# Input projection in seven block products per pair of feature tiles, five down-projection blocks and four input buffers in the mixer, in a one-core encoder layer

## The chip, the cores and the metric

One core of a Trainium2 chip runs the whole layer in one launch. The metric is the device time of an execution in microseconds; the comparison goes by the median of several runs. All arithmetic is in fp32; a matmul in full precision is made from three matmuls in fp32r (a rounded form), each operand being split into a rounded part `hi` and a rest `lo` (hi·hi + hi·lo + lo·hi).

## The reference

2176 frames (2048 of a prompt, and 8 sequences of 16 sample frames) of 1024 features go through one layer:

```python
h = rms_norm(x, g_mix_pre)
qa, ka, va, qb, kb, vb, ga, gb = split(h @ w_in)          # 1024 -> 4352 columns
qa, ka = rope(qa), rope(ka)
oa = attention A (8 query heads, 2 key heads, window of 2 chunks back, sinks)
ob = attention B (8 heads, 8 chunks back, relative-position bias)
mixed = sigmoid(ga) * (oa @ w_oa) + sigmoid(gb) * (ob @ w_ob)
x = x + rms_norm(mixed @ w_out, g_mix_post)
h = rms_norm(x, g_ffn_pre)
u, val = split(h @ w_up)                                  # 1024 -> 2 * 2816
ff = (gelu(causal_conv3(u)) * val) @ w_down               # 2816 -> 1024
x = x + rms_norm(ff, g_ffn_post)
```

The outputs are the frames, and new keys, values and convolution rows.

## The kernel before, in words

Features lie on partitions, frames on the free axis. A matmul multiplies a weight tile of 128x128 with up to 512 frames and adds into a PSUM bank; `mm3` (L127 to L131) issues the three fp32r matmuls of one 128-deep step. `split` (L133) makes `hi` on ScalarE (ACT, L134) and `lo` on VectorE (DVE, L135). All loads and nearly all stores are issued on SyncE's (SP's) one queue.

The stages, in order:

1. **Input projection** (L180 to L373). The 4352 output columns are 34 tiles of 128 (`u`): 0 to 4 values, 5 and 6 to 9 the keys and queries of mixer A (with `rope`), 10 to 13 keys and 14 to 17 queries of mixer B, 18 to 33 the gates. The frames stand in five groups of 512, 512, 512, 384 and 256 (`GROUPS`). The raw frames are split; the weights are scaled by `g_mix_pre` while they are split (`unit` with `g`, L154, L155); the reciprocal norm `rs` multiplies the result when it leaves PSUM (`project`, L196). Each `u` and group takes 8 steps of 128, which are 24 matmuls. The gates of the last two groups (`LATE`, 640 frames) are left for the attention. An evacuated tile of keys or queries is rotated (L324 to L327), scaled (L345), split into `hi` and `lo` (one buffer each) and stored with four DMAs (L304, L312).
2. **Attention** (L378 to L778). Its matmuls are interleaved with those of the late gates as filler (`late_gates`), 256 steps of three matmuls: `F0` of them at the start, `FD` at each of 32 places of the sample part, `F1` after it, the rest by a share, `FE` of which are kept for the end.
3. **Mixer and output projection** (L783 to L960): per frame group, eight tiles `od` are loaded and split (`ot`, two buffers, L816), and eight weight units of `wo` follow; then `w2`.
4. **Up projection** (L963 to L1077). Pairs of feature tiles (gate and value) and two halves of a frame block form a 2x2 block product, made with **seven** block products: `stationary` makes sums of weight tiles on GpSimd (POOL, L982 to L985), `moving` makes sums of frames, `seven` runs 7 products of 12 matmuls over 364 frames in the order `ORDER` into three PSUM banks, and combinations on ACT and DVE give the four results.
5. **Down projection** (L1081 to L1155): six half blocks of 364 or 360 frames (`halves`); per block 22 tiles `gx` are loaded and split into `ghl` (33 buffers), and for each of 8 output tiles 22 steps run; the weights are loaded and split anew for each block. `finish_half` normalises and stores.

The order in which instructions stand on each engine is chosen by a scheduler when the program is built. It keeps each engine's queue in one order; an engine waits at the instruction that stands next.

```python
GROUPS = [(0, 512), (512, 512), (1024, 512), (1536, 384), (1920, 256)]
...
for u in range(3, 34):
    w = wp.unit(i["w1"][u], g=gv[:, 0])
    for g in range(5):
        if u < 18 or g not in LATE:
            evac(u, g, project(w, g, psm, ev))
```

## Time and profile before

| | before |
|---|---|
| median of 3 runs | 3182.87 us (3181.53 to 3184.79) |
| profiled execution | 3180.94 us, span 3178.9 us |
| busy: PE / DVE / ACT / POOL | 3067.4 / 2013.1 / 1391.3 / 517.8 us |
| PE busy, share of the span | 96% |
| mean granted TensorE clock | 0.988 |
| bytes moved | 463.39 MB, mean 146 GB/s |

PE is TensorE's matmul, PEld its weight load. The PE duration of a matmul includes its way through the array, so that neighbours overlap; what a matmul costs is the distance from its start to the next one's. A granted clock of 1.00 is TensorE's upper level of 2.4 GHz, 0.50 the lower of 1.2 GHz. A time behind `<-` is idle time of an engine and what ended it.

### The profile page before, as it was taken

The page shows a single profiled execution, that of the slowest core. Times are in us where ns is not written, and L with a number is a line of the kernel's source. Part 1 is how long each engine was busy: PE and PEld are TensorE (multiplying, and loading weights), DVE is VectorE, ACT ScalarE, POOL GpSimd, SP SyncE. Part 2 cuts the span into 40 slices and gives each one's busy share as a digit, 9 for nine tenths or more (in the row PEclk, how much of TensorE's full clock was granted, in tenths as well). Part 3 has the DMA queues.
Part 4 walks back from the last instruction along what each step waited for, and adds up shares of the span by engine and source line. Part 5 has one row for each costly group of instructions (what it writes and reads, how often), then busy time and mean ns, then how long its engine had stood idle before and what let it go on. Part 6 is the DMA issues. An engine that isn't in the chain of part 4 may idle for free.

```text
span 3178.9 us, 49235 instructions
## 1 busy us (share of the span) xinstructions
PE 3067.4 (96%) x18387; PEld 2810.9 (88%) x18387; DVE 2013.1 (63%) x3769; ACT 1391.3 (44%) x2724; POOL 517.8 (16%) x442
## 2 busy tenths in 40 slices
PE   7999999999999999999979998999989999999997
PEld 6888888888787776899969998999989999999997
DVE  7365442224587665556888878887887775555554
ACT  6264222223587663134444444444444434444432
POOL 0000000001121100000024344434544430000000
PEclk9999999999999999999999999999999999999998
DMA  6366642227766636654533222322222236666764
GB/s 182 93 173 176 142 117 83 82 81 249 236 182 175 169 101 195 217 167 130 155 119 114 105 96 89 126 106 97 86 93 105 103 114 213 217 209 203 213 183 134
DMA packets 253943, 463.39 MB, mean 146 GB/s; under 512 B 29824, under 2 KB 130056, under 8 KB 253704
## 3 DMA queue, kind: packets, MB, share of 16 engines
q1 hardware_dynamic: 249352, 446.62, 45.8%
q0 software_dynamic: 4352, 13.64, 1.2%
q8 instruction: 144, 2.36, 0.3%
q14 instruction: 95, 0.78, 0.1%
HBM read 344.98 MB, written 115.15 MB: 145 GB/s over the span
## 4 chain that ended last, share of the span: by engine, by line
PE 74%; DVE 10%; POOL 5%; ACT 4%; issue 3%; DMA 3%; SPq 0%; POOLq 0%; ACTq 0%; DVEq 0%
PE psm L129 20%; PE psm L131 20%; PE psm L130 19%; PE pso L698 4%; PE pst L715 3%; PE pss L653 2%; POOL ws L983 2%; DMA x<-in_xT 1%; DVE wlo L135 1%; DVE cv L1044 1%; POOL ws L985 1%; POOL ws L982 1%; POOL ws L984 1%; ACT sw L324 1%; PE psf L129 1%
## 5 line engine op out<-in xcount | busy, mean ns | idle before, releaser
L135 DVE TENSOR_TENSOR wlo<-wraw,whi 128x1024 fp32r<-128x1024 f32 (+1 forms) x226 | 300.8, 1332 | 329.6 <-ACT whi L134 328.7
L134 ACT CAST whi<-wraw 128x1024 fp32r<-128x1024 f32 (+1 forms) x226 | 226.9, 1005 | 449.8 <-PE psm L130 325.4
L129 PE MATMUL psm<-hh,whi 128*128 128x512 f32 (+2 forms) x1104 | 408.6, 370 | 12.1 <-ACT hh L134 10.8
L130 PE MATMUL psm<-hl,whi 128*128 128x512 f32 (+2 forms) x1104 | 408.9, 370 | 1.6 <-DVE hl L135 1.6
L131 PE MATMUL psm<-hh,wlo 128*128 128x512 f32 (+2 forms) x1104 | 408.4, 370 | 0.0
L129 PE MATMUL psm<-ghl,whi 128*128 128x364 f32 (+1 forms) x1056 | 349.2, 331 | 2.6 <-ACT ghl L134 2.6
L130 PE MATMUL psm<-ghl,whi 128*128 128x364 f32 (+1 forms) x1056 | 346.5, 328 | 2.1 <-DVE ghl L135 2.1
L131 PE MATMUL psm<-ghl,wlo 128*128 128x364 f32 (+1 forms) x1056 | 347.1, 329 | 0.4 <-DVE wlo L135 0.4
L129 PEld LDWEIGHTS psm<-hh,whi 128*128 128x128 f32 x1104 | 208.6, 189 | 44.4 <-ACT hh L134 10.8
L196 DVE TENSOR_TENSOR f<-psm,rs 128x512 f32<-128x512 f32 (+2 forms) x138 | 87.6, 637 | 245.4 <-PE psm L131 242.5
L130 PEld LDWEIGHTS psm<-hl,whi 128*128 128x128 f32 x1104 | 208.4, 189 | 34.1 <-DVE hl L135 2.1
L131 PEld LDWEIGHTS psm<-hh,wlo 128*128 128x128 f32 x1104 | 208.5, 189 | 32.3 <-issue 0.5
L129 PEld LDWEIGHTS psm<-ghl,whi 128*128 128x128 f32 x1056 | 199.3, 189 | 4.4 <-ACT ghl L134 3.5
L130 PEld LDWEIGHTS psm<-ghl,whi 128*128 128x128 f32 x1056 | 199.1, 189 | 3.3 <-DVE ghl L135 2.7
L131 PEld LDWEIGHTS psm<-ghl,wlo 128*128 128x128 f32 x1056 | 199.4, 189 | 0.7 <-DVE wlo L135 0.7
L982 POOL TENSOR_TENSOR ws<-wraw 128x512 f32<-128x512 f32 x66 | 93.6, 1419 | 564.4 <-DVE wlo L135 438.8
L154 ACT ACTIVATE whi<-wraw,gv 128x128 fp32r<-128x128 f32 x400 | 126.7, 390 | 96.4 <-PE psm L130 75.6
L129 PE MATMUL psm<-mhi,whi 128*128 128x272 f32 x512 | 150.7, 294 | 0.0
L131 PE MATMUL psm<-mhi,wlo 128*128 128x272 f32 x512 | 148.1, 289 | 0.0
L130 PE MATMUL psm<-mlo,whi 128*128 128x272 f32 x512 | 147.6, 288 | 0.0
L1044 DVE SCALAR_TENSOR_TENSOR cv<-ue,cw,cv 128x728 f32<-128x728 f32 (+1 forms) x132 | 130.9, 991 | 2.4 <-ACT cv L1041 1.1
L655 DVE CUSTOM_DVE_ANT_0 pB<-pss,bt 128x640 f32<-128x640 f32 (+4 forms) x128 | 93.8, 737 | 54.9 <-PE pss L653 36.8
(268 smaller groups left out, 8042.8 us busy)
## 6 DMA issues: line engine op xcount, KB each, us to landing
wraw<-in_wu SPq DMA_DIRECT2D x132, 512.0 KB, 3.9
wraw<-in_wd SPq DMA_DIRECT2D x96, 512.0 KB, 3.8
wraw<-in_w SPq DMA_DIRECT2D x58, 512.0 KB, 3.9
keys<-kd SPq DMA_DIRECT2D x80, 256.0 KB, 4.4
wraw<-in_wd SPq DMA_DIRECT2D x48, 384.0 KB, 3.3
q<-qd SPq DMA_DIRECT2D x64, 256.0 KB, 3.8
gd<-cv SPq DMA_DIRECT2D x44, 364.0 KB, 2.3
gx<-gd SPq DMA_DIRECT2D x88, 182.0 KB, 4.1
```

The source lines that it names most:

```text
L129: TE.matmul(ps, lhsT=hi, rhs=xhi, start=first, stop=False, skip_group_check=more)
L130: TE.matmul(ps, lhsT=hi, rhs=xlo, start=False, stop=False, skip_group_check=more)
L131: TE.matmul(ps, lhsT=lo, rhs=xhi, start=False, stop=last, skip_group_check=more)
L134: S.copy(out=hi, in_=src)
L135: E.tensor_sub(out=lo, in0=src, in1=hi.bitcast(F32))
L154: S.activation(out=hi[:, k], in_=r[:, k], func=AF.Copy, scale=g[:, k:k + 1])
L196: V.tensor_mul(out=f, in0=ps, in1=rs[:, t0:t0 + n])
L655: V.tensor_tensor_reduce(out=pj[:, a:], in0=ps[:, off + a:off + 640], in1=bt_[p, hf][:, a:], op0=ALU.add, op1=ALU.min, scale=1.0, scalar=3 ...
L698: TE.matmul(ps_o[hf * HD:(hf + 1) * HD, q0 * P:(q0 + nq) * P], lhsT=v[:, hf * HD:(hf + 1) * HD], rhs=tsb[hf][:, col:col + nq * P], start=( ...
L715: TE.transpose(out=tp[:, col:col + P], in_=u["P"][hf][j][:, bl * P:(bl + 1) * P], identity=ident)
L982: G.tensor_add(out=s1, in0=r1[:, 0:4], in1=r1[:, 4:8])
L1044: V.scalar_tensor_tensor(out=cv[:, :npr], in0=ue[:, s_:s_ + npr], scalar=cw[:, f, s_:s_ + 1], in1=cv[:, :npr], op0=ALU.mult, op1=ALU.add)
```

## The change

1. The input projection is made of the same seven block products as the up projection. Two feature tiles (`u`, `u + 1`) and two halves of a frame block form a pair. The blocks are 2 x 384, 2 x 384 and 2 x 320 frames (`IBLOCKS`). The four value tiles 0 to 3 of the first block are made directly, as before (`DIRECT`), while the block's frames are prepared. Pairs of blocks 0 and 1 cover all 34 tiles, those of block 2 tiles 0 to 17; its gates stay late, over two halves of 320 frames (`LATES`).
2. The frames are scaled by `g_mix_pre` and the reciprocal norm in the staging (`squares`, `norm`, `scale`), so weights are split without a scale and results leave PSUM without one. `moving1` makes the seven sums of frames.
3. Stores are cut at multiples of 512 frames (`segments`), since the scratch tensors are still in chunks of 512. `hi`, `lo`, `cs`, `sn`, `sw` have one buffer each, `f` has five.
4. The down projection has five blocks, four of 464 and one of 320 frames (`DBLOCKS`), 27 buffers `ghl`, six `xh`; `gd` is one tensor per feature tile.
5. The mixer's `ot` has four buffers. The filler is spread by `F0, FD, F1, FE = 64, 3, 4, 56` (72, 3, 8, 40 before).

`stationary` and `seven` move to the front of the program; `seven` gets its PSUM pool and order as arguments. The core of the diff:

```diff
-F0, FD, F1, FE = 72, 3, 8, 40
+F0, FD, F1, FE = 64, 3, 4, 56
+DBLOCKS = [(0, 464), (464, 464), (928, 464), (1392, 464), (1856, 320)]
+DW = 464
-GBUFS = 33
+GBUFS = 27
 ORDER = ((1, 0), (6, 1), (5, 2), (7, 1), (2, 0), (4, 1), (3, 2))
+IBLOCKS = [(0, 384), (768, 384), (1536, 320)]
+IORDER = ((1, 0), (5, 2), (6, 1), (7, 1), (2, 0), (4, 1), (3, 2))
+DIRECT = 4
+LATES = ((1536, 320), (1856, 320))
...
+        def store_q(h0, h1, t0, n, hi, lo):
+            for t, m, c in segments(t0, n):
+                if t >= SEQ:
+                    continue
+                for hf, h in ((0, h0), (1, h1)):
+                    for z, x in ((0, hi), (1, lo)):
+                        dma(out=qd[h][t // 512][z * HD:(z + 1) * HD, t % 512:t % 512 + m],
+                            in_=x[hf * HD:(hf + 1) * HD, c:c + m].bitcast(F32))
...
+        def stage(bi):
+            b0, n = IBLOCKS[bi]
+            hs, ss, r = tiles_of(bi)
+            for c0 in range(0, 2 * n, P):
+                piece(hs, b0, c0)
+            yield hs
+            for c0 in range(0, 2 * n, P):
+                squares(hs, c0, ss)
+                yield hs
+            for z in range(2):
+                norm(ss, z * n, n, r)
+            yield hs
+            for k in range(0, KD, 2):
+                scale(hs, 0, 2 * n, r, (k, k + 1))
+                yield hs
...
+        def moving1(hs, n, pool_of, extra):
...
+            put(1, b11)
+            V.tensor_sub(out=b11, in0=b12, in1=b11)
+            put(5, b11)
+            yield x
+            V.tensor_sub(out=b11, in0=b22, in1=b11)
+            put(6, b11)
+            if extra:
+                put(0, b12)
+            G.tensor_sub(out=b12, in0=b22, in1=b12)
+            put(7, b12)
+            put(2, b21)
+            G.tensor_sub(out=b11, in0=b21, in1=b11)
+            put(4, b11)
+            put(3, b22)
+            yield x
...
+            def ready(z, ps):
+                if z == 0:
+                    S.copy(out=s1, in_=ps[0])
+                elif z == 2:
+                    V.tensor_add(out=q, in0=ps[1], in1=s1)
+                elif z == 3:
+                    V.tensor_add(out=t, in0=ps[1], in1=s1)
+                    f = tile_f()
+                    V.tensor_add(out=f, in0=ps[2], in1=t)
+                    evac(u + 1, tb, n, f)
+                elif z == 4:
+                    f = tile_f()
+                    S.copy(out=f, in_=ps[0])
+                    evac(u, ta, n, f)
+                elif z == 5:
+                    f = tile_f()
+                    V.tensor_add(out=f, in0=ps[1], in1=s1)
+                    evac(u + 1, ta, n, f)
+                elif z == 6:
+                    f = tile_f()
+                    V.tensor_add(out=f, in0=ps[2], in1=q)
+                    evac(u, tb, n, f)
+            seven(w, x, n, ready, psm, IORDER)
...
-            nxt = wp.unit(i["w1"][18], g=gv[:, 0])
+            nxt = wp.unit(i["w1"][18])
...
-        op = ph.enter_context(tc.tile_pool(name="p3i", bufs=2, reuse_waits="tile"))
+        op = ph.enter_context(tc.tile_pool(name="p3i", bufs=4, reuse_waits="tile"))
...
-        for z, (bi, hf) in enumerate(halves):
+        for z, (t0, n) in enumerate(DBLOCKS):
```

The scheduler lays the instructions out anew. Three places follow; a tile's name stands ahead of the arrow, what it is made from behind it.

SP's queue, in the tiles of mixer A's queries (`cs` and `sn` are the rotation's factors, `qd` the stored queries, `wraw` a weight tile that comes in). Before:

```order
L319 DMA cs<-in_cos 128x512
L320 DMA sn<-in_sin 128x512
L304 DMA qd_1_61<-hi 64x512
L304 DMA qd_1_61<-lo 64x512
L304 DMA qd_1_77<-hi 64x512
L304 DMA qd_1_77<-lo 64x512
L319 DMA cs<-in_cos 128x384
L320 DMA sn<-in_sin 128x384
```

In the changed kernel, two results of a pair of the first block:

```order
L299 DMA cs<-in_cos 128x384
L300 DMA sn<-in_sin 128x384
L189 DMA wraw<-in_w 128x1024
L284 DMA qd_0_68<-hi 64x128
L284 DMA qd_0_68<-lo 64x128
L284 DMA qd_0_84<-hi 64x128
L284 DMA qd_0_84<-lo 64x128
L284 DMA qd_1_69<-hi 64x256
L284 DMA qd_1_69<-lo 64x256
L284 DMA qd_1_85<-hi 64x256
L284 DMA qd_1_85<-lo 64x256
```

A result that lies across a multiple of 512 frames is stored with eight DMAs instead of four, and a weight load stands among them.

DVE's queue, same tiles (`f` is the result, `sw` its swapped halves, `lo` the rest that is stored, `wlo`, `wlob`, `wloc` rests of weights, `sq`, `ss`, `nv`, `nt`, `r` the norm of frames). Before:

```order
L325 TENSOR_TENSOR f<-f,cs 128x512
L326 TENSOR_TENSOR sw<-sw,sn 128x512
L327 TENSOR_TENSOR f<-f,sw 128x512
L345 TENSOR_SCALAR f<-f 128x512
L135 TENSOR_TENSOR lo<-f,hi 128x512
L196 TENSOR_TENSOR f<-psm,rs 128x384
```

In the changed kernel:

```order
L305 TENSOR_TENSOR f<-f,cs 128x384
L306 TENSOR_TENSOR sw<-sw,sn 128x384
L144 TENSOR_TENSOR wlo<-wraw,whi 128x1024
L307 TENSOR_TENSOR f<-f,sw 128x384
L144 TENSOR_TENSOR wlob<-wraw,whib 128x512
L323 TENSOR_SCALAR f<-f 128x384
L144 TENSOR_TENSOR wlo<-ws,whi 128x1024
L144 TENSOR_TENSOR wloc<-ws,whic 128x1024
L144 TENSOR_TENSOR lo<-f,hi 128x384
L305 TENSOR_TENSOR f<-f,cs 128x384
L306 TENSOR_TENSOR sw<-sw,sn 128x384
L445 TENSOR_TENSOR f<-psm_1497,s_1493 128x384
```

All four splits of a pair's weights now stand between the steps of the results of another pair.

SP's queue at the mixer's start (`od` is the attention's output, `sgd` the gates). Before:

```order
L816 DMA ot<-od_203 128x512
L816 DMA ot<-od_204 128x512
L830 DMA ga<-sgd_187 128x512
L831 DMA gb<-sgd_195 128x512
L149 DMA wraw<-in_wo 128x1024
L816 DMA ot<-od_205 128x512
L816 DMA ot<-od_206 128x512
L149 DMA wraw<-in_wo 128x1024
```

In the changed kernel:

```order
L158 DMA wraw<-in_wo 128x1024
L993 DMA ot<-od_203 128x512
L993 DMA ot<-od_204 128x512
L993 DMA ot<-od_205 128x512
L993 DMA ot<-od_206 128x512
L1007 DMA ga<-sgd_187 128x512
L993 DMA ot<-od_207 128x512
L1008 DMA gb<-sgd_195 128x512
L993 DMA ot<-od_208 128x512
L993 DMA ot<-od_209 128x512
```

Four `ot` now stand in a row, and all eight stand ahead of the weight loads that follow.

## Rows read from the trace of the kernel before

**Rows 1.** Stretches of the program: length, busy time by engine, clock, DMA.
```profile
core 0: us, PE busy (x) PEld busy (x) DVE busy (x) ACT busy (x) POOL busy (x), PEclk, DMA share, GB/s
0.00:110.00 110.00, 93.22 (x462) 76.90 (x463) 74.93 (x156) 60.80 (x105) 0.71 (x6) 1.00 0.56 164
110.00:480.00 370.00, 368.68 (x1888) 321.71 (x1888) 176.67 (x388) 137.89 (x306) 1.85 (x2) 1.00 0.57 142
...
718.00:1214.00 496.00, 493.06 (x3738) 388.80 (x3736) 319.10 (x1008) 309.68 (x871) 65.96 (x159) 1.00 0.60 179
```

**Rows 2.** Timeline of PE, input projection, first matmul of a group: start, duration.
```profile
334.78 0.33 PE L129 MATMUL psm<-hh,whi 128*128 128x384 f32 x1
338.96 0.28 PE L129 MATMUL psm<-hh,whi 128*128 128x256 f32 x1
341.83 0.40 PE L129 MATMUL psm<-hh,whi 128*128 128x512 f32 x1
358.18 0.33 PE L129 MATMUL psm<-hh,whi 128*128 128x384 f32 x1
```

**Rows 3.** A stretch of the up projection, columns as in rows 1.
```profile
2080.00:2160.00 80.00, 80.00 (x480) 80.00 (x479) 64.47 (x82) 36.12 (x46) 31.86 (x21) 1.00 0.30 106
```

**Rows 4.** Timeline of DVE, first 20 us: the frames' and weights' preparation.
```profile
7.67 0.68 DVE L249 TENSOR_TENSOR sq<-sq 128x512 f32<-128x512 f32 x1
8.28 2.18 DVE L155 SCALAR_TENSOR_TENSOR wlo<-wraw,gv,whi 128x128 fp32r<-128x128 f32 x8
10.38 0.41 DVE L249 TENSOR_TENSOR sq<-sq 128x256 f32<-128x256 f32 x1
10.83 0.29 DVE L250 TENSOR_TENSOR ss<-sq 128x128 f32<-128x128 f32 x1
11.04 1.22 DVE L135 TENSOR_TENSOR hl<-x,hh 128x1024 fp32r<-128x1024 f32 x1
```

**Rows 5.** DVE by line and form, 110 to 480 us: busy, mean ns, idle before.
```profile
L196 DVE TENSOR_TENSOR f<-psm,rs 128x384 f32<-128x384 f32 x15 | 8.3, 555 | 10.7 <-PE psm L131 10.3
L345 DVE TENSOR_SCALAR f<-f 128x384 f32<-128x384 f32 x8 | 2.9, 358 | 0.2
```

**Rows 6.** Instructions on `wraw`: duration min/median/max, ns.
```profile
L135 DVE TENSOR_TENSOR wlo<-wraw,whi x226: 950/1225/2320, 1026.0 to 3148.9; 128x1024 fp32r<-128x1024 f32 x89, 128x768 fp32r<-128x768 f32 x24
L135 DVE TENSOR_TENSOR wlob<-wraw,whib x66: 674/1331/1778, 1645.1 to 2592.4; 128x512 fp32r<-128x512 f32 x66
```

**Rows 7.** Timeline of DVE, change of block in the up projection.
```profile
1962.98 2.31 DVE L135 TENSOR_TENSOR x5l<-hst,x5h 128x1456 fp32r<-128x1456 f32 x1
1978.18 1.66 DVE L135 TENSOR_TENSOR x4l<-xt,x4h 128x1456 fp32r<-128x1456 f32 x1
```

**Rows 8.** The same change of block on PE: idle time and its releaser.
```profile
1955.21 0.44 PE L129 MATMUL psm<-x7h,whic 128*128 128x364 f32 x1 [1.03 <-DVE q L1028]
1963.11 0.43 PE L129 MATMUL psm<-x3h,whic 128*128 128x364 f32 x1 [2.27 <-DVE vv L1031]
1978.40 0.67 PE L129 MATMUL psm<-x6h,whi 128*128 128x364 f32 x1 [5.66 <-ACT whi L134]
```

**Rows 9.** Who waited for whom, 110 to 480 us: total, times, longest.
```profile
ACT hi L134 <- DMA kd<-hi: 46.3, 15, 5.0
DVE lo L135 <- DMA kd<-lo: 41.8, 17, 4.2
```

**Rows 10.** Timeline of ACT, keys: three splits into `hi` in a row.
```profile
318.60 0.62 ACT L134 CAST hi<-f 128x512 fp32r<-128x512 f32 x1 [3.38 <-DMA kd<-hi]
322.32 0.62 ACT L134 CAST hi<-f 128x512 fp32r<-128x512 f32 x1 [3.10 <-DMA kd<-hi]
```

**Rows 11.** Timeline of SP's issues, keys.
```profile
342.56 1.09 SPq L312 DMA_DIRECT2D kd<-hi  x2
```

**Rows 12.** A stretch from attention to mixer, columns as in rows 1.
```profile
1215.00:1230.00 15.00, 8.94 (x19) 5.82 (x20) 9.00 (x12) 5.61 (x7) 0.00 (x0) 0.57 0.83 266
```

**Rows 13.** A stretch from up to down projection, columns as in rows 1.
```profile
2620.00:2630.00 10.00, 5.57 (x23) 4.34 (x22) 7.44 (x17) 4.64 (x9) 0.00 (x0) 0.83 0.47 141
```

More of the change, by code (lines that the diff above doesn't have):

```diff
@@ new lines, in seven @@
+    def seven(w, x, n, evac, bank_pool, order):
+        ps = [bank_pool.tile([P, 512], F32, name="psm3")[:, :n] for _ in range(3)]
+        began = set()
+        for z, (name, bank) in enumerate(order):
+            (whi, wlo), (xhi, xlo) = w[name], x[name]
+            for k in range(4):
+                mm3(ps[bank], whi[:, k], wlo[:, k], xhi[:, k], xlo[:, k],
+                    k == 0 and bank not in began, k == 3, bank in began)
+            began.add(bank)
+            evac(z, ps)
+    hlate = ctx.enter_context(ExitStack())
@@ new lines, in rope @@
+        def rope(f, t0, n):
+            cs = ev.tile([P, IW], F32, name="cs")[:, :n]
+            sn = ev.tile([P, IW], F32, name="sn")[:, :n]
+            dma(out=cs, in_=i["cos"][:, t0:t0 + n])
+            dma(out=sn, in_=i["sin"][:, t0:t0 + n])
+            sw = ev.tile([P, IW], F32, name="sw")[:, :n]
+            for a in range(4):
+                b = a ^ 1
+                S.copy(out=sw[a * 32:(a + 1) * 32], in_=f[b * 32:(b + 1) * 32])
+            V.tensor_mul(out=f, in0=f, in1=cs)
+            V.tensor_mul(out=sw, in0=sw, in1=sn)
+            V.tensor_add(out=f, in0=f, in1=sw)
@@ new lines, in squares, with norm @@
+        def squares(hs, c0, ss):
+            sq = sp.tile([P, KD, P], F32, name="sq")
+            S.activation(out=sq, in_=hs[:, :, c0:c0 + P], func=AF.Square)
+            for w in (4, 2):
+                V.tensor_add(out=sq[:, 0:w], in0=sq[:, 0:w], in1=sq[:, w:2 * w])
+            V.tensor_add(out=ss[:, c0:c0 + P], in0=sq[:, 0], in1=sq[:, 1])
+        def norm(ss, c0, n, r):
+            pn = psn.tile([P, 512], F32, name="psn")[:, :n]
+            TE.matmul(pn, lhsT=ones, rhs=ss[:, c0:c0 + n], start=True, stop=True)
+            rstd_of(pn, sp, r[:, c0:c0 + n])
@@ new lines, in moving1, with put @@
+        def moving1(hs, n, pool_of, extra):
+            x = {}
+            def put(z, src):
+                hi = pool_of(z).tile([P, 4, IW if pool_of(z) is not hp2[0] else 320], F32R, name=f"x{z}h")[:, :, :n]
+                lo = pool_of(z).tile([P, 4, IW if pool_of(z) is not hp2[0] else 320], F32R, name=f"x{z}l")[:, :, :n]
+                split(hi, lo, src)
+                x[z] = (hi, lo)
+            b11, b12, b21, b22 = [hs[:, a:a + 4, c:c + n] for a in (0, 4) for c in (0, n)]
+            put(1, b11)
[13 more added lines that the diff above has]
+            yield x
@@ new lines, in encoder_layer @@
+        units = [(bi, u) for bi in range(3) for u in range(DIRECT if bi == 0 else 0, 18 if bi == 2 else 34, 2)]
+        weights = lambda u: stationary(i["w1"][u], i["w1"][u + 1], wx, sx)
+        ws = [weights(units[0][1])]
+        for x in xgen:
+            pass
+        nxt = iter(())
+        seen = 0
+        for z, (bi, u) in enumerate(units):
+            if bi != seen:
+                seen = bi
+                for hs in nxt:
+                    pass
+                n = IBLOCKS[bi][1]
+                if bi == 2:
+                    xr.close()
+                    hp2[0] = hlate.enter_context(tc.tile_pool(name="hp2", bufs=1, side="right", reuse_waits="tile"))
+                    xc = xr.enter_context(tc.tile_pool(name="xc", bufs=1, side="right", reuse_waits="tile"))
+                    xgen = moving1(hs, n, lambda y: hp2[0] if y < 4 else xc, True)
+                else:
+                    xgen = moving1(hs, n, lambda y: xa if y in (1, 5) else xb, False)
+                for x in xgen:
+                    pass
+                nxt = iter(())
+            if z + 1 < len(units):
+                ws.append(weights(units[z + 1][1]))
+            if bi < 2 and u == 8:
+                nxt = stage(bi + 1)
+            hs = next(nxt, hs)
+            if bi < 2 and u > 24:
+                hs = next(nxt, hs)
+            pair(u, bi, ws.pop(0), x)
@@ L378, in encoder_layer @@
+        late.update({g: (x[y], x[y2]) for g, y, y2 in ((0, 1, 2), (1, 0, 3))})
+    xr.close()
     with ExitStack() as ph:
@@ L1084, in encoder_layer @@
         sp = ph.enter_context(tc.tile_pool(name="p5", bufs=2, reuse_waits="tile"))
-        halves = [(bi, z) for bi in range(3) for z in range(2)]
+        np_ = ph.enter_context(tc.tile_pool(name="p5n", bufs=1, reuse_waits="tile"))
         finish = []
```

439 lines of the change are left out of this document (208 added, 231 removed).

## The prediction

> **What bounds the kernel now.** I read the stretches first. In the input projection PE is busy 368.68 of 370 us between 110 and 480 us, in the attention 493.06 of 496; only the first 110 us leave 16.8 us idle [rows 1]. So a matmul less is time less, as long as DVE, ACT, POOL and SP keep up. In those 370 us DVE works 177 and ACT 138 us, less than half [rows 1], but that is a mean: the rows of waits show that DVE and ACT stood 41.8 and 46.3 us behind stores of keys alone, since `hi` and `lo` have one buffer each and the next tile must wait until the last one's stores have landed [rows 9]. Today this hides behind 5.45 us of matmuls for a group of 512. The second view is the distance of matmuls, from the first matmul of one group to the first of the next: 24 of 384 columns take 4.18 us, 0.1742 each; 24 of 256 take 2.87, 0.1196 each; 72 of 512 take 16.35, 0.2271 each [rows 2]. In the up projection 480 of 364 columns take 80 us, 0.1667 each [rows 3]. By interpolation 320 columns cost 0.147 and 464 cost 0.2075.
>
> **The change, part by part.**
>
> *Matmuls of the input projection.* Before: 18 tiles over five groups and 16 over three, 2448 matmuls of 512, 432 of 384, 432 of 256: 555.9 + 75.3 + 51.7 = 682.9 us. After: 192 direct ones and 32 pairs of 84 with 384 columns, 9 pairs of 84 with 320: 2880 x 0.1742 + 756 x 0.147 = 501.7 + 111.1 = 612.8 us. **Minus 70.1 us.** The eighth that the scheme saves is not all there, because a narrow matmul costs more per column (0.454 ns at 384, 0.444 at 512). The Trainium skill ("TensorE: Matmul & The Clock Gate", section "Back-to-back issue gap") states a fixed 2.5 ns above the columns' own time for an isolated matmul; by that the same term would be 75 us, an estimate from that page. The rows have some 13 ns above 512/2.4, 384/2.4 and 256/2.4 [rows 2], and the measured distances decide. The late gates stay 640 frames: 384 x (0.1742 + 0.1196) = 112.8 us before, 768 x 0.147 = 112.9 after; nothing. Their weights are now split in one instruction on each engine instead of eight; that cover is the attention's PE at 493 of 496 us, so it is worth nothing.
>
> *Down projection.* Before 2112 x 0.1667 + 1056 x 0.165 = 526.3 us, after 2112 x 0.2075 + 528 x 0.147 = 515.8: minus 10.5. Its start is fed by loads: in 10 us PE began 23 matmuls where 60 fit, 6.2 us lost [rows 13]; a first block 1.27 times as wide loses some 2 us more (bounds 0 and 6). With 27 buffers instead of 33 only five tiles of the next block are ready before the last output tile; the other 17 are split while its 66 matmuls run, 0.62 us per step against about 0.63 on DVE; hidden. **Minus 8.5 us.**
>
> *Mixer's start.* PE began 19 matmuls in 15 us where 66 fit, the clock granted 0.57 on average, so part of it at the lower level, 1.2 GHz: 47 x 0.227 = 10.7 us lost [rows 12]. Now four `ot` come in a row ahead of the weights, and 16 more filler steps (7 us) stand at the end. I take **minus 7** (bounds 0 and minus 11). The front filler of 64 steps, 28 us, still covers the way of the last queries to the sample part; if it did not, 5 us.
>
> *The start.* Ahead of the first pair's last products DVE must do: six pieces of frames, each split and summed, 6 x (1.22 + 0.68 + 0.41 + 0.29) = 15.6; four scaled weights of 2.18, 8.7 [rows 4]; two norms of four, eight evacuations and sixteen scalings, 32 x 0.555 = 17.8 [rows 5]; nine operations of 1536 columns, at 1.66 x 1536/1456 = 1.75 each 15.8, at 2.31 beside POOL 21.9 [rows 7]; the pair's weights 3 x 1.225 + 1.33 = 5.0 [rows 6]. Together 63 to 69 us, from some 6.5 us on, with 5 to 8 of waits: about 79 us. PE has by then 192 + 60 matmuls, 44 us, and the transposes, some 5. So it idles some 30 us instead of 16.8 [rows 1]. **Plus 14** (bounds 4 and 25).
>
> *Pairs with keys and queries.* This is the main cost. PE needs 84 x 0.1742 = 14.63 us for a pair of blocks 0 and 1, 12.35 of block 2. DVE needs for a rotated query pair: five combinations and four times three rotation steps and one rest, 21 x 0.555 = 11.7; four scalings 1.4 [rows 5]; weights 5.0 [rows 6]; together 18.1. SP needs 0.54 us per issue [rows 11]: 24 stores (four results, two of them cut in two), 8 factors, 2 weights, 18.4 us. Without rotation DVE needs 11.4 and SP 14.0, but the single `hi` buffer turns round in 3.7 us when nothing else holds it [rows 10], and a cut result issues two more `hi` stores, 4.8: 17.0 us for four results. So an excess of 3.7 us for a rotated pair and 2.4 for another; per block 2.5 rotated (tile 5 is half a pair) and 4 others: 18.9. In blocks 0 and 1 the staging of the next block stands there too, 6 x 1.38 + 8 x 1 + 5 = 21 us of DVE, of which the slack of the four pairs takes 4 x 3.2; 8 remain. Block 2: (2.8 to 3.5 + 2.5) in the same way, 18.8. Sum: 27 + 27 + 19 = 73 us. Not all of it reaches PE: `f` has five buffers, so results may lag by 5 x 3.66 = 18 us in each block, and gate pairs or the filler behind them (DVE 7 of 14.6 us) let them catch up. But the next pair's weights stand in the same queues [the order shown on DVE and SP], and cannot lag. I take 14 of the 18: 73 - 42 = **plus 31** (bounds 19 and 73; today such stalls cost 1.3 us in 370 [rows 1], which bounds it from below at nothing).
>
> *Changes of block.* In the up projection a change leaves PE idle 1.03 + 2.27 + 5.66 us [rows 8]. Here the first two sums have a pool of their own and their DVE instructions stand ahead of the last pair's combinations, so they run under it. **Plus 10** for two (bounds 0 and 25, the latter with the lower clock).
>
> Sum: -70.1 - 8.5 - 7 + 14 + 31 + 10 = -30.6. The profiled execution took 3180.94 us (span 3178.9), the median of the runs is 1.9 above: 3150.3 and **3152 us** in the runs.
>
> **The rivals.**
>
> *A. The stores stay hidden.* If the scheduler's order lets results lag freely, the pairs cost 5 instead of 31 us: 3126 us. For it: today's stores cost PE almost nothing though DVE and ACT wait 88 us for them [rows 1, 9]. Against it: DVE and SP exceed the pair's time by sums, not only by waits.
>
> *B. Slower: the one `hi` and `lo` buffer sets the pace.* Where a weight split stands on DVE behind a rest that waits for a store, PE waits with it, and the lag of `f` is worth nothing. The place is pairs 4 to 17 of each block; the price is 3.7 us a pair, 73 in all: -30.6 + 42 = +11, 3194 us; at 5 us a pair 3219. It decides from (31 + 30.6)/19.5 = 3.2 us per pair on. For it: waits of up to 5.0 us for one landing [rows 9]; against it: the gate pairs, which have no store waits, stand close behind.
>
> *C. POOL slows DVE.* Each pair has four sums on POOL. The same split takes 1.225 us in the median and up to 2.32, and `x5l` 2.31 where `x4l` took 1.66 [rows 6, 7]. If one more of a pair's weight splits runs at 2.3, 19.5 x 1.1 = 21 us more: 3174 us. The Trainium skill ("GPSIMD Engine Reference", section "Key points") says that GpSimd shares its SBUF interfaces with VectorE and contends with DVE instructions that read two tensors from SBUF, as these do; by that rule such splits are slow whenever POOL works, and the rows just named agree.
>
> *D. The narrow matmul is slower in block products than in groups*, so that the 70 us shrink. The up projection's products run at 0.1667 for 364 columns [rows 3], on the line between 256 and 384 [rows 2]; I give it next to nothing, inside the forecast's range.
>
> **How the numbers follow.** A measurement of this kernel tells about 0.2% (6 us) from no change. Forecast 0.50 (3134 to 3168 with the bounds of start, mixer and blocks), A 0.20 (3110 to 3134), C 0.13 (3168 to 3186), B 0.17 (3186 to 3220). Faster: 0.50 + 0.20 + 0.09 of C = 0.79; same: 0.04 of C and 0.01 of B, 0.05; slower 0.16. The range 3120 to 3195 leaves out the lower part of A (0.07) and the upper of B (0.10).
>
> **What would show it.** Right: 3636 matmuls in the input projection at 0.174 and 0.147 us; the attention beginning near 688 us instead of 718; in the first 110 us some 30 us of idle PE; PE waiting for `wlo` and for `f` in pairs 4 to 17, some 1.6 us a pair, and hardly in gate pairs; ACT's `hi` behind DMA `qd` and `kd`; under 5 us at each change of block; the mixer's first 15 us with some 50 matmuls; the down projection near 516 us of matmuls. Wrong: if pairs with queries take over 18 us (B), or gate pairs stall too, which would put the cost on the weights' single buffers; or if PE loses nothing in pairs 4 to 17 (A); or if the start takes more than 90 us before the second pair.

## The result: 3380 us, 6% slower than before

The changed kernel takes 3379.95 us in the median (3377.36 to 3385.44), the one before 3182.2; the ratio is 1.0625, 95% interval 1.0609 to 1.0641. Forecast were 3152 us, in a range of 3120 to 3195, so the result lies outside the range and on the other side. The profiled execution has a span of 3375.6 us, 196.7 more than the one of before. By the first matmul of each stage (the late gates, `ohi`, `mhi`, `ghl`) the time stands so:

| stage | before, us | after, us | difference | forecast |
|---|---|---|---|---|
| input projection | 721.0 | 917.2 | +196.2 | -15 |
| attention with late gates | 493.3 | 502.6 | +9.3 | 0 |
| mixer | 198.7 | 188.7 | -10.0 | -7 |
| output and up projection | 1211.0 | 1214.7 | +3.7 | 0 |
| down projection | 554.9 | 552.4 | -2.5 | -8.5 |

All of the loss is in the input projection. The first view is the stretches, with the columns of [rows 1]; the third is a piece of the pairs with keys of mixer B, the fourth the attention, and the last three are the start of the mixer, the start of the down projection and a piece of the latter, to be held against [rows 1, 12, 13]:

```profile
0.00:110.00 110.00, 81.47 (x416) 76.53 (x417) 82.83 (x132) 57.03 (x95) 28.01 (x20) 0.95 0.44 125
110.00:480.00 370.00, 299.42 (x1519) 283.24 (x1518) 227.85 (x306) 162.13 (x250) 112.64 (x74) 0.89 0.45 132
199.00:233.00 34.00, 25.70 (x116) 25.02 (x117) 15.73 (x26) 8.65 (x13) 5.28 (x4) 0.75 0.41 112
917.20:1419.20 502.00, 496.28 (x3728) 391.16 (x3728) 306.75 (x915) 289.25 (x775) 67.14 (x159) 0.99 0.60 177
1419.00:1434.00 15.00, 13.16 (x55) 10.16 (x56) 12.62 (x19) 9.02 (x13) 0.54 (x1) 1.00 0.94 325
2821.00:2831.00 10.00, 5.82 (x14) 4.25 (x15) 8.10 (x17) 5.71 (x10) 0.00 (x0) 0.66 0.55 182
2900.00:2980.00 80.00, 80.00 (x382) 71.49 (x382) 35.24 (x45) 32.57 (x50) 0.00 (x0) 1.00 0.54 168
```

Between 110 and 480 us PE was busy 368.68 us and is busy 299.42 now, at a clock of 0.89 instead of 1.00. The third row is the one to think about: in 34 us DVE works 15.73, ACT 8.65, POOL 5.28 and PE 25.70 at three quarters of its clock. No engine is the bound. So the engines wait for each other in turn, and the timeline of these microseconds shows the ring. One line per step, of five engines, in order of time (start, duration, engine, line, operation; in brackets the idle time before it and what ended it):

```profile
209.36 0.62 ACT L143 CAST whib<-wraw 128x512 fp32r<-128x512 f32 x1 [3.75 <-PE psm L139]
210.01 0.69 DVE L144 TENSOR_TENSOR wlob<-wraw,whib 128x512 fp32r<-128x512 f32 x1 [3.83 <-ACT whib L143]
210.74 0.33 SPq L190 DMA_DIRECT2D wraw<-in_w  x1
214.46 1.26 POOL L193 TENSOR_TENSOR ws<-wraw 128x512 f32<-128x512 f32 x1 [16.42 <-DMA wraw<-in_w]
218.50 1.04 ACT L143 CAST whi<-ws 128x1024 fp32r<-128x1024 f32 x1 [5.40 <-POOL ws L194]
219.58 1.31 DVE L144 TENSOR_TENSOR wlo<-ws,whi 128x1024 fp32r<-128x1024 f32 x1 [3.45 <-ACT whi L143]
220.82 0.55 DVE L445 TENSOR_TENSOR f<-psm,s 128x384 f32<-128x384 f32 x1
221.42 0.69 PE L138 MATMUL psm<-x1h,whi 128*128 128x384 f32 x1 [7.06 <-DVE f L445]
231.74 0.62 ACT L143 CAST whib<-wraw 128x512 fp32r<-128x512 f32 x1 [1.07 <-PE psm L139]
```

Product 4 (`x4h`), the last but one of a pair, is the only one that reads `whib`, and frees it; only then ACT and DVE split the second weight tile, which frees its `wraw` buffer; only then SP can issue the load for the pair after; 3.7 us later POOL sums, then ACT and DVE split the sums. The result `f` of the pair that PE has finished stands behind that split on DVE, and holds the PSUM bank that PE's next pair needs. The last line is the same step as the first, one pair later: 12.1 us pass from the split of `whib` to PE's start, 10.3 more until PE has done its next product 4. So a turn of the ring takes 22.4 us, with 72 matmuls in it, 12.5 us at the upper clock level. The matmul shown takes 0.69 us where 0.33 is usual, and those next behind it start 0.32 us apart or more instead of 0.1742: after 7.06 us of waiting PE is at 1.2 GHz. By their distances in the timeline some 425 of the 3636 matmuls of the input projection ran at that level, about 60 us lost; the granted clock between 0 and 917 us is 0.90. The waits between 100 and 890 us say the same (who waited for whom: total, times, longest):

```profile
PE psm L138 <- DVE f L445: 30.0, 8, 7.7
PE psm L138 <- ACT whi L143: 24.7, 9, 7.5
ACT whi L143 <- POOL ws L194: 147.5, 35, 7.7
POOL ws L193 <- DMA wraw<-in_w: 471.8, 33, 29.2
SPq L189 <- POOL ws L196: 166.3, 31, 12.3
```

POOL sits idle 472 us behind weight loads, and SP 166 us behind POOL for the buffer to load into: a ring. The up projection, in the same trace, has two buffers for `whib` and `whic` (and one for `ws`, as here), and there both loads of a pair go out together:

```profile
2046.38 0.33 SPq L189 DMA_DIRECT2D wraw<-in_wu  x1
2046.93 0.33 SPq L190 DMA_DIRECT2D wraw<-in_wu  x1
2060.43 0.33 SPq L189 DMA_DIRECT2D wraw<-in_wu  x1
2060.99 0.33 SPq L190 DMA_DIRECT2D wraw<-in_wu  x1
```

That is 14.05 us a pair, which is what its 84 matmuls need [rows 3].

### The profile page after: what moved, and what is told of

It is laid out like the page before. It is cut to its first block, busy times and chain, and to the rows that moved or that the text cites. A ratio compares the mean times of both kernels' runs of the same rounds, so it can differ in the third digit from the quotient of the medians.

```text
span 3375.6 us, 49364 instructions
## 1 busy us (share of the span) xinstructions
PE 3088.3 (91%) x18188; PEld 2848.8 (84%) x18188; DVE 2208.7 (65%) x3672; ACT 1480.0 (44%) x2643; POOL 775.2 (23%) x612
## 4 chain that ended last, share of the span: by engine, by line
PE 56%; DVE 9%; POOL 7%; DMA 5%; issue 4%; ACT 4%; SPq 1%; POOLq 0%; DVEq 0%; ACTq 0%
PE psm L138 14%; PE psm L139 14%; PE psm L140 14%; PE pso L875 3%; PE pst L892 3%; DMA wraw<-in_w 2%; POOL ws L194 2%; PE pss L830 2%; DVE wlo L144 2%; POOL ws L195 2%; POOL ws L193 2%; POOL ws L196 1%; ACT whi L143 1%; DVE cv L1183 1%; PE pss L806 1%
## 5 line engine op out<-in xcount | busy, mean ns | idle before, releaser
L193 POOL TENSOR_TENSOR ws<-wraw 128x512 f32<-128x512 f32 x107 | 148.4, 1387 | 1138.9 <-DMA wraw<-in_w 503.6
L138 PE MATMUL psm<-ghl,whi 128*128 128x464 f32 (+1 forms) x880 | 319.9, 364 | 2.2 <-ACT ghl L143 2.2
L139 PE MATMUL psm<-ghl,whi 128*128 128x464 f32 (+1 forms) x880 | 317.7, 361 | 2.0 <-DVE ghl L144 2.0
L140 PE MATMUL psm<-ghl,wlo 128*128 128x464 f32 (+1 forms) x880 | 316.7, 360 | 0.3 <-DVE wlo L144 0.3
L138 PE MATMUL psm<-x1h,whi 128*128 128x364 f32 (+3 forms) x428 | 149.0, 348 | 40.4 <-DVE f L445 30.0
L196 POOL TENSOR_TENSOR ws<-wraw,ws 128x512 f32<-128x512 f32 x107 | 183.9, 1719 | 8.4
L138 PE MATMUL psm<-x7h,whic 128*128 128x364 f32 (+3 forms) x428 | 152.0, 355 | 34.3 <-DVE q L433 27.9
L194 POOL TENSOR_TENSOR ws<-ws,wraw 128x512 f32<-128x512 f32 x107 | 173.6, 1622 | 0.0
L138 PE MATMUL psm<-x4h,whib 128*128 128x364 f32 (+3 forms) x428 | 148.6, 347 | 27.2 <-DVE t L435 21.1
L138 PE MATMUL psm<-x2h,whi 128*128 128x364 f32 (+3 forms) x428 | 149.8, 350 | 13.8 <-ACT s L431 10.6
L195 POOL TENSOR_TENSOR ws<-wraw 128x512 f32<-128x512 f32 x107 | 155.8, 1456 | 0.0
L140 PE MATMUL psm<-x1h,wlo 128*128 128x364 f32 (+3 forms) x428 | 148.0, 346 | 7.4 <-DVE wlo L144 7.4
```

The costliest lines, as they stand in the source:

```text
L138: TE.matmul(ps, lhsT=hi, rhs=xhi, start=first, stop=False, skip_group_check=more)
L139: TE.matmul(ps, lhsT=hi, rhs=xlo, start=False, stop=False, skip_group_check=more)
L140: TE.matmul(ps, lhsT=lo, rhs=xhi, start=False, stop=last, skip_group_check=more)
L193: G.tensor_add(out=s1, in0=r1[:, 0:4], in1=r1[:, 4:8])
L194: G.tensor_sub(out=s2, in0=s1, in1=r0[:, 0:4])
L195: G.tensor_sub(out=s3, in0=r0[:, 0:4], in1=r1[:, 0:4])
```

## The experiments

All runs stand against 3380 us for the change and 3182 for before. All but 16 and 18 also make the last block's sums `x4` to `x7` 320 wide, for the room, and the scheduler lays every program out anew, so that differences of some 10 us (runs 2, 3, 9) are not read as causes. A pair's length is the distance from its `q` combination on DVE (one per pair, behind its third product) to that of the next. The table has its mean over the 11 pairs with keys and queries of mixer B (no rotation), over the 9 with keys and queries of mixer A (rotated), and its median over the eight gate pairs of the second block. 14.63 us of matmuls is the least at 384 frames, 12.35 in the last block. The columns for mixer B and the rotated pairs depend on where a pair is cut: with the distance from the `q` before, the change has 23.1 and 21.2, run 12 has 19.7 and 20.1.

| run | us | mixer B | rotated | gates |
|---|---|---|---|---|
| the change | 3380.0 | 25.5 | 19.7 | 17.2 |
| 1: two `whib` | 3356.6 | 25.5 | 20.2 | 14.7 |
| 2: two `hi`, `lo` | 3389.6 | 26.0 | 19.7 | 17.0 |
| 3: gate stores on ACT | 3387.7 | 25.3 | 20.1 | 16.5 |
| 4: second weight tile, own two buffers | 3336.6 | 24.5 | 18.2 | 14.7 |
| 5: two `whib`, `whic` | 3331.1 | 24.6 | 20.6 | 14.7 |
| 6: two `ws`, one buffer more for loads | 3361.9 | 24.6 | 20.7 | 14.7 |
| 7: 5 and two `hi`, `lo` | 3370.3 | 20.4 | 25.7 | 14.7 |
| 8: 4 and six PSUM banks | 3340.6 | 24.9 | 18.2 | 14.7 |
| 9: one store per head | 3389.6 | 27.1 | 18.9 | 16.8 |
| 10: 4 and 9 | 3355.0 | 26.7 | 17.5 | 14.7 |
| 11: 10 and two `hi`, `lo` | 3278.8 | 18.5 | 18.9 | 15.1 |
| 12: 7 and 9 | 3267.1 | 16.3 | 23.6 | 14.7 |
| 13: 12 with one `whic` | 3291.3 | 19.1 | 20.8 | 14.8 |
| 14: 13, factors once a block | 3291.5 | 17.0 | 24.2 | 14.7 |
| 15: 12, sums of frames on DVE | 3259.7 | 17.1 | 22.5 | 14.7 |
| 17: 12 without the rotation | 3216.6 | 17.6 | 16.1 | 14.7 |

**Run 1, 4: the weights' ring.** Run 1 gives the second tile's split two buffers, run 4 its load (`rx` is a pool with two buffers):

```diff
-            hi = pool.tile([P, nk, P], F32R, name=f"whi{tag}", tag=f"whi{tag}")
+            nb = {"bufs": 2} if tag == "b" else {}
+            hi = pool.tile([P, nk, P], F32R, name=f"whi{tag}", tag=f"whi{tag}", **nb)
```

```diff
-        r1 = wp.raw.tile([P, 8, P], F32, name="wraw")
+        r1 = (rx or wp.raw).tile([P, 8, P], F32, name="wraw")
```

> The weights' second part `whib`/`wlob` of a pair gets two buffers in the input projection (as in the up projection) instead of one; for the room, the last block's sums `x4` to `x7` are 320 wide instead of 384. Theory W (the single weight buffers close a loop over load, POOL's sums, split and product, longer than a pair): both weight loads of a pair are issued together, gate pairs fall from 16.6 to under 15 us, query pairs too by 2 us or more; the late gates' first matmul comes 60 to 150 us sooner than 917 us, the time is 3220 to 3320 us instead of 3380. Theory S (the single `hi` and `lo` and their stores set the pace): gate pairs alone gain, 20 x 2 us at most, 3340 us or more. Theory Q (stores ahead of weight loads on SP's queue): no gain, 3370 us or more.

> The second weight tile of a pair is loaded into two buffers of its own (and the first keeps two), so that both loads of the next pair need not wait for the splits of this one; for the room, the last block's sums are 320 wide, and the bias table is built in tiles that are there anyway. Theory W: the loop is cut at the load, POOL's waits for weight loads (472 us of idle time between 100 and 890 us) fall to a third or less, gate pairs under 15.2 us, time 3220 to 3320 us. If the split `whib` itself, behind PE's fourth product of the pair before, is what counts: the loads go early, but the gain is under half of the one with two `whib`. Theory S: 3340 us or more. Theory Q: 3360 us or more.

Measured 3356.63 (ratio to before 1.0547, 1.0529 to 1.0564) and 3336.56 us (1.0486, 1.0470 to 1.0501). The gate pairs fall to 14.7 us in both, with PE full; a stretch of gate pairs in run 1:

```profile
293.00:351.00 58.00, 58.00 (x334) 57.38 (x333) 28.66 (x37) 25.11 (x40) 20.30 (x16) 1.00 0.37 126
```

So theory W is shown for the gate pairs. For the others it isn't: the pairs of mixer B keep 25.5 and 24.5 us, and both gains, 23 and 43 us, are under the 60 that were expected at least.

**Runs 2, 3: stores.** Two `hi` and `lo` (run 2); the gates' stores issued by ACT (run 3):

```diff
-            hi = ev.tile([P, IW], F32R, name="hi")[:, :n]
-            lo = ev.tile([P, IW], F32R, name="lo")[:, :n]
+            hi = ev.tile([P, IW], F32R, name="hi", bufs=2)[:, :n]
+            lo = ev.tile([P, IW], F32R, name="lo", bufs=2)[:, :n]
...
-                dma(out=sgd[u - 18][:, t0:t0 + n], in_=f)
+                nc.scalar.dma_start(out=sgd[u - 18][:, t0:t0 + n], in_=f)
```

> `hi` and `lo` get two buffers each instead of one in the input projection. Theory S: waits of ACT's `hi` and DVE's `lo` for DMAs of `qd` and `kd` (39 and 25 us of idle time after 100 us) go, pairs with keys and queries fall from 17 to 29 us to under 18, time 3260 to 3320 us. Theory W: the waits go, but the pairs keep their length within 1.5 us, since weights set it; gate pairs stay at 16.6 us; 3355 us or more. Theory Q: as W.

> The stores of the gates `sgd` are issued on ACT's queue, right behind the sigmoid that makes them, instead of SP's. Theory Q: on SP they wait 79 us in all for the sigmoid, and the load of a pair's second weight tile stands behind them; without them it goes 2 to 7 us sooner, and gate pairs fall from 16.6 to under 15.2 us, 20 of them: 3330 to 3350 us. Theory W: that load waits for its buffer, which `wlob` frees at about the same time: gate pairs 16 us or more, time 3365 us or more.

Measured 3389.56 and 3387.7 us, both some 8 to 10 us slower than the change. Theory Q falls, and so does theory S as long as the weights have single buffers: two `hi` and `lo` alone shorten no kind of pair.

**Runs 5, 6, 8: the rest of the ring.** Run 5 has the first line of these, run 6 the second (and one buffer of its own for the second tile, as in run 4), run 8 is run 4 with the last two:

```diff
-        wx = ph.enter_context(tc.tile_pool(name="wx1", bufs=1))
+        wx = ph.enter_context(tc.tile_pool(name="wx1", bufs=2))
...
-        sx = ph.enter_context(tc.tile_pool(name="sx1", bufs=1))
+        sx = ph.enter_context(tc.tile_pool(name="sx1", bufs=2))
...
-        psm = ph.enter_context(tc.tile_pool(name="psm1", bufs=5, space=PSUM))
-        psv = ph.enter_context(tc.tile_pool(name="psv", bufs=2, space=PSUM))
+        psm = ph.enter_context(tc.tile_pool(name="psm1", bufs=6, space=PSUM))
+        psv = ph.enter_context(tc.tile_pool(name="psv", bufs=1, space=PSUM))
```

> Both `whib`/`wlob` and `whic`/`wloc` get two buffers in the input projection, as in the up projection; the weight tiles keep two buffers as in the change, `f` has four instead of five, for the room. Theory W2 (with the loads early, what is left is the loop through `ws`: the last product of a pair frees `whic`, its split on ACT and DVE frees `ws`, POOL's sums of the next pair but one start then, their split stands on ACT and DVE ahead of results, and PE waits for the PSUM bank of such a result): with `whic` free a pair early, POOL's sums start early; query and key pairs fall from 21 to 27 us to under 18, the time is 3180 to 3280 us, against 3337 with the loads alone mended. If the stores of `hi` and `lo` set the pace of these pairs: the gates alone gain, 3330 us or more. If `f` with four buffers is too few: PE waits for results longer, no gain.

> `ws`, the sums of a pair's weights, gets two buffers, and the second weight tile one buffer of its own (the first keeps two); `whib` and `whic` stay single, `f` has four buffers. Theory W2: POOL's wait for `wloc` (400 us of idle time with the loads alone mended) goes; pairs with queries and keys under 18 us, time 3180 to 3290 us. If the split `whib` or `whic` behind PE's last products is what holds the results on ACT and DVE: under 20 us of gain against 3337 us. If the stores set the pace: 3330 us or more.

> As the run with two buffers of its own for the second weight tile, and six PSUM banks for the pairs instead of five (one for the transposes of values instead of two), so that two pairs fit. Theory P (PE waits because a result that stands behind a weight split on DVE holds a PSUM bank; a sixth bank lets the next pair start): PE's waits for `f` and `q` (61 us after 100 us) halve, 3290 to 3320 us against 3337. Theory W2: the splits of the weights are late themselves, PE then waits for `whi` and `wlo` instead: within 12 us of 3337.

Measured 3331.09, 3361.93 and 3340.63 us. W2 and P fall: no buffer of the weights, and no PSUM bank, brings the pairs of mixer B under 24 us. But with the weights in time the trace of run 5 shows what holds them now, ACT's splits of results into `hi`:

```profile
230.38 0.52 ACT L143 CAST hi<-f 128x384 fp32r<-128x384 f32 x1
237.23 0.51 ACT L143 CAST hi<-f 128x384 fp32r<-128x384 f32 x1 [3.40 <-DMA kd<-hi]
244.28 0.51 ACT L143 CAST hi<-f 128x384 fp32r<-128x384 f32 x1 [0.79 <-DMA qd<-hi]
248.25 0.51 ACT L143 CAST hi<-f 128x384 fp32r<-128x384 f32 x1 [2.25 <-DMA qd<-hi]
251.60 0.51 ACT L143 CAST hi<-f 128x384 fp32r<-128x384 f32 x1
```

Four results take 21.2 us: a cut one, with eight stores, holds the buffer 7 us, a whole one 3.4 to 4. Three of the four splits that follow the first wait for the DMA of the one before. That is rival B, hidden behind the first ring.

**Run 7: both rings, all stores.** The edits of runs 5 and 2 together.

> As the run with two buffers for `whib` and `whic`, and two for `hi` and `lo` too; for the room `f` has three buffers and `vk` one. Theory S in its second form (once the weights come in time, the stores of keys and queries are next): 20 to 60 us less than without the second `hi` and `lo`. Theory W2: within 15 us of it either way.

Measured 3370.28 us, 39 more than run 5 where 20 to 60 less were expected. The pairs of mixer B do get shorter, but SP's queue is the next bound. Run 7, SP (the second line is the last of 56 stores in a row, in 38 us), and PE behind it:

```profile
210.44 0.59 SPq L293 DMA_DIRECT2D kd<-hi  x1
211.08 0.59 SPq L293 DMA_DIRECT2D kd<-lo  x1
211.77 0.53 SPq L189 DMA_DIRECT2D wraw<-in_w  x1
...
216.90 0.69 PE L138 MATMUL psm<-x1h,whi 128*128 128x384 f32 x1 [12.75 <-ACT whi L143]
```

With two buffers the scheduler puts the stores of many results one behind the other, 0.64 us apart, and the next pair's weights behind them all. `f` and `vk` have fewer buffers here too; run 12, with the same ones, shows that they are not the cost.

**Runs 9 to 12: half the stores.** `hi` and `lo` lie in one tile, and one DMA stores both for a head:

```diff
-                    for z, x in ((0, hi), (1, lo)):
-                        dma(out=kd[h0 + hf][t // 512][:, z, t % 512:t % 512 + m],
-                            in_=x[hf * HD:(hf + 1) * HD, c:c + m].bitcast(F32))
+                    dma(out=kd[h0 + hf][t // 512][:, :, t % 512:t % 512 + m],
+                        in_=hl[hf * HD:(hf + 1) * HD, :, c:c + m].bitcast(F32))
```

> The change with `hi` and `lo` of a result in one tile, stored by one DMA per head instead of two: two stores a result (four where it is cut) instead of four (eight). Weights as in the change. Theory SP (a pair of keys or queries needs two cut and two whole results, each of which holds the single `hi` and `lo` for 7 and 4 us until its stores, issued 0.6 us apart on SP, have landed: 22 us a pair; and weight loads stand behind them): with half the stores 20 to 70 us less than 3380. Theory W (the weights' single buffers alone count as long as they are single): under 15 us less.

> Two buffers of its own for the second weight tile (3337 us by itself) and one DMA per head for `hi` and `lo`. Theory SP: pairs of keys fall from 22 to 15 to 17 us, query pairs to under 20, 3240 to 3300 us. Otherwise, if the loop through `wloc`, `ws` and POOL holds the pairs with keys: 3320 us or more.

> As the run with two buffers of its own for the second weight tile and one DMA per head, and two buffers for `hi` and `lo`; `vk` has one buffer, for the room. Theory SP: with the stores halved the second buffer costs nothing, as it did with all the stores in the queue (3370 against 3331 us): 3220 to 3290 us, and within 20 us of the run with one buffer. If a second `hi` and `lo` hurts by itself (results further behind): 20 us or more slower than with one.

> Two buffers for `whib` and `whic`, two for `hi` and `lo`, one DMA per head, three `f` and one `vk`: the run that took 3370 us, with half the stores. Theory SP (there, 24 stores stood in a row on SP, 0.64 us apart, ahead of the next pair's weights): 60 to 120 us less than 3370. If `f` with three buffers was its cost: 3350 us or more.

Measured 3389.63, 3355.01, 3278.77 and 3267.05 us (run 12: 1.0274, 1.0259 to 1.0289). Runs 9 and 10 miss what theory SP expected, run 12 meets it, run 11 meets it in its time but not in its distance from run 10. Half the stores are worth nothing alone, and nothing with the loads alone mended (run 10 against 4: 18 us slower); a second `hi` and `lo` on top is worth 76 us (11 against 10); and what cost 39 us in run 7 becomes a gain of 64 over run 5 with half the stores. Three changes, of which none gives over 50 us by itself, give 113 together, with the weights' buffers of run 5. The pairs of mixer B in run 12, and its gate pairs:

```profile
191.00:266.00 75.00, 70.62 (x390) 68.60 (x389) 58.83 (x75) 35.11 (x53) 26.23 (x18) 0.98 0.61 173
286.00:329.00 43.00, 42.81 (x246) 42.18 (x245) 23.42 (x26) 18.11 (x29) 17.86 (x12) 1.00 0.37 128
```

390 matmuls of 0.1742 us are 67.9 of the 75 us, where the change's row had 116 in 34 us, 20.2.

**Runs 13, 14, 15, 17: what is left.** Run 13 is run 12 with `whic` single, four `f` and two `vk`. The cores of runs 14 (on 13), 15 and 17 (on 12):

```diff
-            dma(out=cs, in_=i["cos"][:, t0:t0 + n])
-            dma(out=sn, in_=i["sin"][:, t0:t0 + n])
+            if b0 not in factors:
+                factors[b0] = [ev.tile([P, 2 * IW], F32, name=z)[:, :2 * m] for z in ("cs", "sn")]
+                for x, z in zip(factors[b0], ("cos", "sin")):
+                    dma(out=x, in_=i[z][:, b0:b0 + 2 * m])
...
-            G.tensor_sub(out=b12, in0=b22, in1=b12)
+            V.tensor_sub(out=b12, in0=b22, in1=b12)
...
-            G.tensor_sub(out=b11, in0=b21, in1=b11)
+            V.tensor_sub(out=b11, in0=b21, in1=b11)
...
-            if u < 10:
-                rope(f, t0, n)
```

> Two buffers for `whib` alone (`whic` single), two for `hi` and `lo`, one DMA per head, `f` with four buffers. Theory WS (the weights' loop and the stores' loop each hold the pairs, so that either mended alone gains little and both together gain over 100 us; of the weights' buffers `whib` is the one that counts): 3260 to 3295 us. If `whic` counts as much: 3300 us or more.

> As the run with two `whib` and halved stores, and the factors `cs` and `sn` of the rotation loaded once per block of frames instead of once per result, and two buffers for `sw`. Theory R (a rotated result goes one by one through the load of its factors, four copies on ACT and three steps on DVE, some 6 us, four times a pair, 25 us against 14.6 or 12.4 us of matmuls; 2.5 pairs a block): 25 to 60 us less than without. If DVE's work itself (18 us a rotated pair) is the limit: 5 to 20 us less. If neither: within 5 us.

> As the run with two `whib` and `whic` and halved stores, and the two sums of frames that `moving1` makes on POOL (4.5 and 7.1 us at a block change, with the weights' sums behind them and DVE's splits waiting) made on DVE (1.75 us each by its splits of the same width). Theory B (the block changes lose 19 to 21 us each to the chain of sums and splits, POOL's part 12 us of it): 10 to 25 us less than 3267. If DVE is the limit there: within 5 us or slower.

> As the run at 3267 us (two `whib` and `whic`, halved stores), with the rotation of the keys and queries of mixer A left out (no factors, no copies on ACT, no rotation steps on DVE; their values are then not the reference's). Theory R2 (in that run the stretches with rotated pairs lose 35, 22 and 36 us, 93 in all, to the rotation's way over DMA, ACT and DVE): 50 to 90 us less, 3177 to 3217. If the stores or the weights hold these pairs too: under 30 us less, 3237 or more.

Measured 3291.27, 3291.5, 3259.72 and 3216.6 us. Theory WS holds; the single `whic` costs 24 us (the `f` and `vk` differ too). Loading the factors once changes nothing in the sum (R falls). The two sums on POOL cost 7 us in all, below the 10 to 25 of theory B; the two changes of block lose 40 us in run 12 and 38 in run 15. The rotation as a whole is worth 50 us, at the lower end of R2. Run 14 speaks against the loads of its factors, though on a kernel with a single `whic`; the copies on ACT or the steps on DVE are then left, and which of them was not separated. In run 12 the rotated pairs of the last block look like this, PE at 39 of 66 us and DVE at 43:

```profile
722.00:788.00 66.00, 39.09 (x204) 36.34 (x203) 43.46 (x70) 32.42 (x64) 17.54 (x13) 0.77 0.57 158
```

Still 34 us above before remain in run 17, which leaves work out; in which parts of start, changes of block and the last pairs, was not taken apart further.

**Runs 16, 18: the other parts alone, on the kernel before.** Run 16 has the five down blocks, four `ot` and the new spread of the filler, with the old input projection; run 18 only `ot` and filler.

```diff
-F0, FD, F1, FE = 72, 3, 8, 40
+F0, FD, F1, FE = 64, 3, 4, 56
...
-        op = ph.enter_context(tc.tile_pool(name="p3i", bufs=2, reuse_waits="tile"))
+        op = ph.enter_context(tc.tile_pool(name="p3i", bufs=4, reuse_waits="tile"))
```

> The kernel before, with the other parts of the change alone: five down blocks with 27 buffers, four input buffers in the mixer, and the filler's new spread; the input projection is the old one. By the stages of the changed kernel (mixer 188.7 us against 198.6, down 554 against 557, attention 502 against 496): 6 to 14 us less than before, 3168 to 3177. By the prediction's terms (-7 and -8.5): 3167. If the attention's 6 us come from the filler's spread and not from the late gates' new width: 3173 to 3180.

> The kernel before with four `ot` in the mixer and the filler's new spread alone. From the run with both other parts (12.5 us less than before): 8 to 11 us less than before if the mixer's start is worth what the stretches show (10 us) and the down blocks 2 to 4; by the prediction's terms 7, and 5.5 to 8.5 for the down blocks.

Measured 3168.79 us (0.9960, 0.9947 to 0.9972) and 3172.27 (0.9971, 0.9960 to 0.9981). **Run 16 beats both kernels**, the one before by 12.5 us, which is 0.4%: some 9 to 10 from the mixer's `ot` and the filler together (run 18), and 3 from the down blocks, a part that the intervals of the two runs don't tell from nothing. Its mixer start has 64 matmuls in 15 us, against 19 [rows 12]:

```profile
1215.00:1230.00 15.00, 14.39 (x64) 11.85 (x64) 13.00 (x18) 8.97 (x12) 0.54 (x1) 1.00 0.94 324
```

Its attention lasts 494.9 us from the first late gate to `ohi` against 493.3 before, so of the 9.3 us that the changed kernel loses there at most 1.6 come with the filler, the rest with the new late gates or what precedes them.

## Why the prediction was wrong

*Matmuls of the input projection: right.* Forecast 612.8 us; 2880 of 0.1742 and 756 of 0.147 stand in the trace where PE is at the upper level, and where PE isn't held (gate pairs in run 1) a pair takes 14.67 us.

*The start: right.* PE is idle 28.5 of the first 110 us, against 16.8: plus 12, forecast plus 14.

*Mixer: right,* 55 matmuls in its first 15 us, where about 50 were forecast, and 10 us by the stages (9.8 in run 18, with the filler) for 7. *Down projection: too much.* 382 matmuls of 464 columns in 80 us are 0.2094 each, where interpolation gave 0.2075, 4 us; and its start has 14 of 48 matmuls in 10 us, 7.1 us lost instead of 6.2, so 0.9 more where 2 were allowed. Gained were 2.5 to 3.5 us instead of 8.5; some 3 us of the shortfall stay open.

*Changes of block: wrong,* at 10 us for two. From the start of the last gate pair to the end of the second pair of the next block 70 and 67 us pass (358 to 428 and 706 to 773), with 44 and 39 us of matmuls: 54 us lost, some 5 of them to transposes of value tiles, which PE makes too. The bound of 25 was taken from the up projection's change [rows 8]. But the sums here stand between single weight buffers: with two `whib` and `whic` the two changes lose 41 us (run 5), so these buffers are 12 of the 54. POOL's two sums, which the prediction put no price on, last 4.45 and 7.13 us at the first change, with the next pair's weight sums behind them; making them on DVE gave 7 us (run 15). What makes the 38 us that remain in run 15 was not tried. POOL and PE at the first change:

```profile
370.38 4.45 POOL L413 TENSOR_TENSOR hst<-hst 128x1536 f32<-128x1536 f32 x1
385.72 7.13 POOL L416 TENSOR_TENSOR hst<-hst 128x1536 f32<-128x1536 f32 x1 [10.89 <-DVE x6l L144]
392.81 1.27 POOL L193 TENSOR_TENSOR ws<-wraw 128x512 f32<-128x512 f32 x1
...
399.16 0.69 PE L138 MATMUL psm<-x5h,whi 128*128 128x384 f32 x1 [7.50 <-ACT whi L143]
```

*Gate pairs: wrong.* They were to let the results catch up, at no cost; they took some 17 us themselves, and lost 26 us in all (276 to 358 and 609 to 706 us). The prediction had named stalls in gate pairs as the sign that the weights' single buffers are the cost, and runs 1, 4 and 5 bear that out; but in its sum it priced them at nothing.

*Pairs with keys and queries: the step that failed.* The prediction took a pair's length as the largest of four sums, PE 14.63, DVE 18.1, SP 18.4, the turns of `hi` 17.0, and let 42 of the 73 us of excess vanish in the five `f`. Measured are 25.5 us without rotation and 19.7 with it. The stretches of values, keys and queries (110 to 276, 428 to 609, 773 to 917 us) hold 310 us of matmuls and last 491: 181 lost, some 2 of it to transposes; forecast 31. In all, the input projection loses 304 us beyond its 612.8 us of matmuls, where the one before lost 38. Four things were wrong in that step. First, the largest of the sums is the length only if the engines can run apart; with one buffer at each of `whib`, `whic`, `ws`, `hi` and `lo`, and two `wraw` for a pair that needs both, the waits add up along the ring. The row at 199 to 233 us shows it: PE, waiting, is the busiest with 76%, and a turn takes 22.4 us. Second, `f` can't lag, as what it waits behind on DVE is the next pair's weight split, which itself is late. The prediction saw this order, and that weights cannot lag, and allowed 14 us a block all the same. Third, the price of a cut result was 4.8 us for two more `hi` stores; in run 5 it is 7 us, since `lo` stores stand among those of `hi` on SP. Fourth, the sum priced every matmul at the upper clock level; the waits put some 425 of them on the lower one, about 60 of the 304 us. Rival B had the place and the sign right, but the price of 3.7 us a pair is the smaller part: with 11 and 5 us a pair it fell short as well.

*Attention and up projection: not foreseen,* plus 9.3 and 3.7 us. In the attention PE is idle 6.3 us instead of 2.4, and its first 12.8 us (from 917.2 on) have a granted clock of 0.77, some 3 us; what makes the rest was not tried.

Of the rivals, A is excluded. C, POOL slowing DVE, was not tried by itself, but the change's trace bounds it: up to 917 us 57 of DVE's instructions that overlap POOL's take over 1.2 times as long as their like do without POOL (none of the others does), 51 us of DVE's 552 in all; only 9 of the 199 splits into `wlo`, `wlob` and `wloc` are among them, 7 us, where C had one a pair. How much of the 51 us reaches PE is not shown. D is excluded by the 14.67 us of the gate pairs.
